# Hybrid decoder step: the value half of the gated MLP projected with stationary weights, and brought back to tokens by 32x32 transposes and DRAM

## The chip, the cores and the metric

The kernel runs on one core of one Trainium2 chip. Its time is the device time of one execution in microseconds (us). The core has five instruction streams: TensorE (PE; its weight loads are shown apart as PEld), VectorE (DVE), ScalarE (ACT), GpSimd (POOL) and SyncE (SP). Each works through its own list in order, and they wait for each other by semaphores. DMA transfers are issued from the lists of SP, ACT and POOL.

## The reference

One layer over 320 tokens (256 of a prompt, 64 of eight samples), width 2048, float32. What matters here is the input projection and the gated MLP:

```python
h = rms_norm(x, p["norm_mix_pre"])
proj = h @ p["w_in"]            # columns: gMLP u | gMLP v | SSD z | SSD x,B,C | SSD dt
...
u = jax.nn.gelu(a_u, approximate=False)
v = layer_norm(jax.nn.gelu(a_v, approximate=False), ln_g, ln_b)   # over 2048 columns
s = jnp.einsum("hts,bnshd->bnthd", w, vp) + b_s ...               # mixes tokens of a chunk
return u * s, v[:, start:]
```

`a_v` is h times 2048 columns of `w_in`. Its layer norm runs over columns, and the spatial gate contracts over tokens, so the kernel wants v with tokens on the partitions: `vt`, 128 partitions x 3 chunks of tokens (128, 128 and 64) x 2048 columns. Everything else it keeps with columns on the partitions and the 320 tokens along the free dimension.

## The kernel before

**Products in three parts.** A float32 operand is split in two, a rounded high part and the residue (hi, lo), and a product is the sum of three matmuls: high x high, low x high, high x low. x comes with columns on the partitions; `h_hi` and `h_lo` hold its parts for all 16 blocks of 128 input columns (`kt`).

**Weights.** `slab` (L109) loads up to 128 x 1024 weights (512 KB) on SP's queue into `wraw`; ACT casts them to `whi` (L123) and DVE makes the residue `wlo` (L124). Each of the three tiles has three buffers. A load therefore waits until the residue of the slab three back is made, and a cast until PE is done with the slab three back. `wraw` is shared with two loads of the dt columns (`wraw_dt`, `dt_columns`).

**The usual projection.** `project` (L194) takes 512 columns at a time: four PSUM banks, one per block of 128 columns; weights stationary (128x128), 320 tokens streaming; 3 x 16 matmuls of 320 per block (`accumulate`, L150 to L155). A block is evacuated by a callback when its last matmul is made. There are four banks with the tag `mm`, so a block of the next project waits for the evacuation of the block of the same number.

**The projection of v.** It comes first in the program, and the other way round: tokens stationary, weights streaming. `by_tokens` (L131, matmuls at L143) makes for each `kt` and each half (n = 0, 1; 1024 columns each) 16 matmuls of 512 columns: two chunks of 128 tokens x two groups x three products, and for the 64 tokens of the samples two matmuls per group with both parts of x side by side (`xs_two`, 2 x 64 columns, made by DVE at L646), one of them with 64 stationary columns. PSUM holds 3 x 2 banks per half. At the end of a half ACT takes Gelu straight from PSUM into `vt`, scaled by the RMS factor of each token (L721); for the samples DVE first adds the two parts (L719, L720). The first half (n = 0) runs while x arrives. In the same steps `x_ready` (L634) splits x (ACT L639, DVE L640), `x_squares` (L648) squares it on ACT (L651) and adds on DVE (L653), `root` makes the RMS factor r, and `dt_products` (L518) projects dt. In the second half `spread` turns r into r1 (one row per partition), and `params` loads `prm` and `sst` on SP.

**After v.** B, C and the first heads (`conv_proj`, L460) are projected with the usual `project`. Beside them `layer_norm` (L727) runs in pieces: `bn_stats` on 512 columns at a time (L734), `bn_aggr`, and two passes over `vt` (L752, L753), 24 in all. `gate_mix` (L765) then uses `vt` as stationary operand (L786).

**What sets the order.** Background work is written as generators. `tick` is called after each part of a `project`; it advances every task in `side` and the first in `bg`. What a generator yields is the number of matmuls until it may go on. A scheduler then orders each engine's list by priorities (`first()` and `high_priority` go ahead; `issue_after` holds an instruction behind another one). `pv` is a tag with four buffers of 128 x 320, shared by several short-lived tiles; `vf` has two of 128 x 4 x 320.

## Time and profile before

| | |
|---|---|
| Runs, us | 1768.35, 1768.94, 1769.97 (median 1768.94) |
| The profiled execution, us | 1768.21 |
| Its span, first to last instruction, us | 1766.5 |
| Mean granted TensorE clock | 0.999 |
| PE busy | 1754.9 us (99%) |
| DVE, ACT, POOL busy | 1171.0, 823.7, 286.4 us |
| First v matmul, first matmul of B | 5.42 us, 128.24 us |

In a row of a group of instructions stand the line in the kernel, the engine, the operation, the tiles as out<-in, the shapes and the count; behind the bar the busy time in us, the mean duration of one in ns, and the idle time of the engine ahead of it with what ended it. Matmuls are pipelined: the next one starts while the one before is still in flight, so a duration says how long one is in flight, and the distance of the starts what one costs. In a row of waits stand who waited, for whom, the us in total, the times, and the longest. In a row of a window stand the stretch, the busy time and count of PE, PEld, DVE, ACT and POOL, the granted clock, the share of time in which the DMA engines were busy, and GB/s. In a row of DMA issues stand out<-in, the queue, the count, the size of one, and the median us from issue to landing.

### The profile page before, as it was taken

How to read it: one execution, taken by the hardware profiler on the slowest of the kernel's cores; microseconds unless marked ns; L12 is line 12 of the kernel's file. 1: busy time of each engine (PE TensorE's matmuls, PEld its weight loads, DVE VectorE, ACT ScalarE, POOL GpSimd, SP SyncE). 2: the span in 40 equal slices, each digit the busy share in tenths (PEclk: the TensorE clock that was granted, in tenths of full speed). 3: DMA queues.
4: the chain of work that ended last, by engine and by line, in shares of the span. 5: the costliest groups of instructions: out<-in, count | busy, mean ns of one | idle time of the engine just before them, and what ended most of it. 6: DMA issues, size and time to landing. Idle time of an engine off the chain costs nothing.

```text
span 1766.5 us, 30627 instructions
## 1 busy us (share of the span) xinstructions
PE 1754.9 (99%) x11873; PEld 1708.2 (97%) x11873; DVE 1171.0 (66%) x2020; ACT 823.7 (47%) x1200; POOL 286.4 (16%) x627
## 2 busy tenths in 40 slices
PE   9999999999999999999999999999999999999998
PEld 7789999999899999999999999999999999999998
DVE  7549774656869777788855565665657565656575
ACT  5434555333655575655645434343434343333445
POOL 1202220000313222112211111010202010101004
PEclk9999999999999999999999999999999999999999
DMA  7556655455676766665654545554554545454542
GB/s 261 161 153 169 192 167 160 149 153 156 213 224 181 238 199 210 199 208 162 186 155 146 157 146 157 146 157 146 156 148 154 150 152 150 153 156 145 155 152 103
DMA packets 221051, 296.97 MB, mean 168 GB/s; under 512 B 19945, under 2 KB 147305, under 8 KB 220713
## 3 DMA queue, kind: packets, MB, share of 16 engines
q1 hardware_dynamic: 208568, 274.61, 51.5%
q10 hardware_dynamic: 9584, 13.38, 2.1%
q0 software_dynamic: 2752, 7.02, 1.4%
q8 instruction: 94, 1.54, 0.4%
q14 instruction: 53, 0.43, 0.1%
HBM read 277.88 MB, written 17.07 MB: 167 GB/s over the span
## 4 chain that ended last, share of the span: by engine, by line
PE 60%; DVE 0%; ACT 0%; issue 0%; ACTq 0%
PE ps L153 12%; PE ps L155 12%; PE ps L154 12%; PE pd L155 7%; PE pd L154 7%; PE pd L153 7%; PE x1p L1381 0%; PE fin_ps L1111 0%; PE y_ps L1039 0%; PE tsum L311 0%; PE ps_one L153 0%; PE ps_one L155 0%; PE ps_one L154 0%; PE ps_other L153 0%; PE ps_other L155 0%; PE ps_other L154 0%
## 5 line engine op out<-in xcount | busy, mean ns | idle before, releaser
L124 DVE TENSOR_TENSOR wlo<-wraw,whi 128x1024 fp32r<-128x1024 f32 (+1 forms) x476 | 582.6, 1224 | 427.0 <-ACT whi L123 424.7
L123 ACT CAST whi<-wraw 128x1024 fp32r<-128x1024 f32 (+1 forms) x475 | 494.7, 1042 | 676.2 <-PE ps L154 333.3
L153 PE MATMUL ps<-h_hi,whi 128*128 128x320 f32 x2268 | 700.7, 309 | 1.0 <-ACT whi L123 0.7
L155 PE MATMUL ps<-h_hi,wlo 128*128 128x320 f32 x2268 | 698.6, 308 | 0.7 <-DVE wlo L124 0.7
L154 PE MATMUL ps<-h_lo,whi 128*128 128x320 f32 x2268 | 699.1, 308 | 0.0
L153 PEld LDWEIGHTS ps<-h_hi,whi 128*128 128x128 f32 x2268 | 425.5, 188 | 4.1 <-issue 1.2
L155 PEld LDWEIGHTS ps<-h_hi,wlo 128*128 128x128 f32 x2268 | 425.5, 188 | 1.0 <-DVE wlo L124 1.0
L154 PEld LDWEIGHTS ps<-h_lo,whi 128*128 128x128 f32 x2268 | 425.7, 188 | 0.4
L155 PE MATMUL pd<-fhi,wlo 128*128 128x320 f32 x704 | 217.0, 308 | 0.0
L153 PE MATMUL pd<-fhi,whi 128*128 128x320 f32 x704 | 217.0, 308 | 0.0
L154 PE MATMUL pd<-flo,whi 128*128 128x320 f32 x704 | 217.0, 308 | 0.0
L153 PE MATMUL pd<-ohi,whi 128*128 128x320 f32 x448 | 138.9, 310 | 1.3 <-DVE pad L474 1.3
L155 PE MATMUL pd<-ohi,wlo 128*128 128x320 f32 x448 | 138.3, 309 | 0.0
L154 PE MATMUL pd<-olo,whi 128*128 128x320 f32 x448 | 138.3, 309 | 0.0
L153 PEld LDWEIGHTS pd<-fhi,whi 128*128 128x128 f32 x704 | 132.1, 188 | 0.0
L154 PEld LDWEIGHTS pd<-flo,whi 128*128 128x128 f32 x704 | 132.1, 188 | 0.0
L155 PEld LDWEIGHTS pd<-fhi,wlo 128*128 128x128 f32 x704 | 132.1, 188 | 0.0
L1283 POOL COPY ptf<-pad 128x2 f32<-128x2 f32 x88 | 21.0, 238 | 600.0 <-DVE pad L1271 599.4
L266 DVE TENSOR_TENSOR acc_ffn<-acc_ffn,pd 128x320 f32<-128x320 f32 (+1 forms) x161 | 77.5, 482 | 37.8 <-PE pd L155 36.4
L153 PEld LDWEIGHTS pd<-ohi,whi 128*128 128x128 f32 x448 | 84.1, 188 | 2.4 <-issue 1.3
L154 PEld LDWEIGHTS pd<-olo,whi 128*128 128x128 f32 x448 | 84.1, 188 | 0.3
L155 PEld LDWEIGHTS pd<-ohi,wlo 128*128 128x128 f32 x448 | 84.1, 188 | 0.0
(337 smaller groups left out, 1868.0 us busy)
## 6 DMA issues: line engine op xcount, KB each, us to landing
wraw<-in_ffn_w_up SPq DMA_DIRECT2D x176, 512.0 KB, 3.7
wraw<-in_w_in SPq DMA_DIRECT2D x140, 512.0 KB, 3.8
wraw<-in_ffn_w_down SPq DMA_DIRECT2D x88, 512.0 KB, 3.4
wraw<-in_w_out SPq DMA_DIRECT2D x64, 512.0 KB, 3.4
st<-in_state_ssm SPq DMA_DIRECT2D x40, 256.0 KB, 4.8
out_ssm_state_sample<-st ACTq DMA_DIRECT2D x30, 256.0 KB, 2.6
cs<-dacs_d SPq DMA_DIRECT2D x16, 320.0 KB, 5.1
xr<-in_xT SPq DMA_DIRECT2D x4, 640.0 KB, 4.1
```

The costliest lines, as they stand in the source:

```text
L123: rounded[:] = [act.copy(hi, raw).ins]
L124: dve.tensor_tensor(out=lo, in0=raw, in1=hi.bitcast(F32), op=ALU.subtract)
L153: pe.matmul(ps, whi, xhi, start=first, stop=False)
L154: pe.matmul(ps, whi, xlo, start=False, stop=False)
L155: last_made[0] = pe.matmul(ps, wlo, xhi, start=False, stop=last).ins
L266: added_last[:] = [dve.tensor_tensor(out=acc[:, nb, ts], in0=acc[:, nb, ts], in1=ps[:, ts], op=ALU.add).ins]
L1283: pool.tensor_copy(ptf[:, k, :], pad[:, 256:258])
```

## The change

v is projected like everything else: weights stationary, the 320 tokens streaming, as 16 blocks of 128 columns in 3 x 16 matmuls each. `by_tokens`, `banks` and `xs_two` go.

- The first six blocks (768 columns) take the place of the first half, beside the arrival of x. A slab is 768 columns wide (two of 384 in the first four steps), and a step has 18 matmuls of 320. The six banks are four of `mm` and two of `ms`.
- The other ten blocks are two projects of 512 columns and one of 256.
- `v_out` evacuates a block: DVE transposes its 32x32 squares from PSUM into `turned` (two tiles of the tag `vf`, each for two pairs of blocks). After every second block POOL stores the pair to DRAM (`v_d`) in four DMAs, one for each 32 partitions, with runs of 64 floats.
- `v_in`, a task in `side`, loads a pair back with tokens on the partitions (`v_rows`, tag `pv`, three DMAs on POOL). 48 matmuls later three Gelus on ACT (one per chunk of tokens) write 256 columns of `vt` in their right order, and after every second pair DVE makes `bn_stats` of 512 columns.
- `spread`, `params` and the first step of the dt task become a background task. `layer_norm` waits until `v_in` is done, and then makes `bn_aggr` and its two passes as before.

In the changed kernel lines move: the cast and the residue stay at L123 and L124, the three products are L134 to L136, h_lo is L622, the adds of squares L633, the Gelu of v L679, the transposes L657, the stores L661 and the loads L675.

**DVE in the x stage.** Rows of DVE's list before, from the residue of kt = 6 to that of kt = 8 (wlo is a slab's residue, h_lo that of x, acc_mix the sum of squares, w_dt the scaled dt columns):

```order
L124 TENSOR_TENSOR wlo<-wraw,whi 128x1024
L640 SCALAR_TENSOR_TENSOR h_lo<-vt,h_hi 128x320
L646 COPY xs_two<-h_hi 128x64
L653 TENSOR_TENSOR acc_mix<-acc_mix 128x640
L646 COPY xs_two<-h_lo 128x64
L653 TENSOR_TENSOR acc_mix<-acc_mix 128x640 x2
L124 TENSOR_TENSOR wlo<-wraw,whi 128x1024
L640 SCALAR_TENSOR_TENSOR h_lo<-vt,h_hi 128x320
L646 COPY xs_two<-h_hi 128x64
L510 TENSOR_TENSOR w_dt<-wraw_dt,vt 128x256
L646 COPY xs_two<-h_lo 128x64
L124 TENSOR_TENSOR wlo<-wraw,whi 128x1024
```

In the changed kernel, from the residue of kt = 7 to that of kt = 10:

```order
L124 TENSOR_TENSOR wlo<-wraw,whi 128x768
L622 SCALAR_TENSOR_TENSOR h_lo<-vt,h_hi 128x320
L492 TENSOR_TENSOR w_dt<-wraw_dt,vt 128x256
L124 TENSOR_TENSOR wlo<-wraw,whi 128x768
L622 SCALAR_TENSOR_TENSOR h_lo<-vt,h_hi 128x320
L633 TENSOR_TENSOR acc_mix<-acc_mix 128x640 x3
L124 TENSOR_TENSOR wlo<-wraw,whi 128x768
L622 SCALAR_TENSOR_TENSOR h_lo<-vt,h_hi 128x320
L633 TENSOR_TENSOR acc_mix<-acc_mix 128x640
L124 TENSOR_TENSOR wlo<-wraw,whi 128x768
```

The copies into xs_two are gone, the residues are 768 wide, and three adds of squares with an h_lo now stand directly ahead of the residue of kt = 9.

**ACT where v's Gelus stand.** Before, from the last casts of the first half (the Gelus read PSUM, `ps_v`, or the sample sums in `acc_mix`):

```order
L123 CAST whi<-wraw 128x1024 x3
L721 ACTIVATE vt<-ps_v,rs_r 128x512 x4
L123 CAST whi<-wraw 128x1024
L721 ACTIVATE vt<-acc_mix,rs_r 64x512 x2
L123 CAST whi<-wraw 128x1024 x3
L321 COPY r_115<-spread 128x320
L123 CAST whi<-wraw 128x1024 x12
L721 ACTIVATE vt<-ps_v,rs_r 128x512 x4
```

In the changed kernel, from the first cast of the seventh block on (the Gelus read `v_rows`, which a DMA brings):

```order
L123 CAST whi<-wraw 128x1024 x4
L302 COPY r_123<-spread 128x320
L123 CAST whi<-wraw 128x1024 x6
L679 ACTIVATE vt<-v_rows,rs_r 128x256 x2
L679 ACTIVATE vt<-v_rows,rs_r 64x256
L679 ACTIVATE vt<-v_rows,rs_r 128x256
L123 CAST whi<-wraw 128x1024
L679 ACTIVATE vt<-v_rows,rs_r 128x256
L679 ACTIVATE vt<-v_rows,rs_r 64x256
L123 CAST whi<-wraw 128x1024 x2
L679 ACTIVATE vt<-v_rows,rs_r 128x256 x2
L679 ACTIVATE vt<-v_rows,rs_r 64x256
```

Two groups of six Gelus of 512 columns have become eight groups of three of 256, each between weight casts; the chunks of the second pair stand on both sides of a cast.

**POOL behind the first blocks.** Before, from the clearing of vt's sample rows on (`lg` and `lb` are the rows of the layer norm's weights, `r_there` marks r1):

```order
L713 MEMSET vt 64x2048
L471 COPY pad<-sst 128x8x3 x3
L405 COPY r_there<-r_115 128x1
L745 DMA lg<-in_gate_ln_g 128x512
L745 DMA lb<-in_gate_ln_b 128x512
L524 COPY dtf<-dtf 128x64
L526 COPY dtf<-dtf 128x128 x2
L745 DMA lg<-in_gate_ln_g 128x512
L745 DMA lb<-in_gate_ln_b 128x512
```

In the changed kernel, from the same place on (`v_d_106` is the first pair in DRAM, `v_d_107` the second):

```order
L724 MEMSET vt 64x2048
L661 DMA v_d_106<-turned 32x10x64 x4
L661 DMA v_d_107<-turned 32x10x64 x4
L661 DMA v_d_108<-turned 32x10x64 x4
L675 DMA v_rows<-v_d_106 128x256 x2
L675 DMA v_rows<-v_d_106 64x256
L387 COPY r_there<-r_123 128x1
L506 COPY dtf<-dtf 128x64
L508 COPY dtf<-dtf 128x128 x2
L675 DMA v_rows<-v_d_107 128x256
L760 DMA lg<-in_gate_ln_g 128x512
L661 DMA v_d_109<-turned 32x10x64
```

Twelve stores and the first loads of v now stand ahead of r_there, and the later stores and loads stand between the loads of lg and lb.

The diff, cut to its core:

```diff
+    v_d = [dr.tile([NT, 2 * P], F32, name=f"v_d{i}") for i in range(KD // 2)]
...
-                        for i in range(2):
-                            dve.tensor_copy(xs_two[kt // 8][:, kt % 8, NS * i:NS * i + NS], hT[i][:, kt, NP:])
...
-            for n in range(2):
-                ps = banks("ps_v")
-                for kt in range(KD):
-                    x = [h[:, kt, :] for h in hT], xs_two[kt // 8][:, kt % 8, :]
...
-                        wb = slab(rows_of(w_in, kt, 1, cs, 1024))
-                        by_tokens(ps, *x, [wb(0, g, 512) for g in range(2)], (0, 1), kt == 0, kt == KD - 1)
...
+            turned = [gp.tile([P, 4, NT], F32, tag="vf", name="turned", bufs=2).rearrange("p j n -> p (j n)") for _ in range(2)]
+            turned = [t[:, 2 * NT * h:2 * NT * h + 2 * NT].rearrange("p (s j f) -> p s j f", j=2, f=32) for t in turned for h in range(2)]
+            v_there = []
+
+            def v_out(b, ps):
+
+                t = turned[b // 2 % len(turned)]
                 with first():
-                    for c, g in ((0, 0), (0, 1), (1, 0), (1, 1), (2, 0), (2, 1)):
-                        at, src = slice(0, NS if c == 2 else P), ps[c][g]
-                        if c == 2:
-                            src = acc[:, 2 + 2 * g:4 + 2 * g, :].rearrange("p k n -> p (k n)")[:NS, :512]
-                            dve.tensor_copy(src, ps[2][g][NS:])
-                            dve.tensor_tensor(out=src, in0=src, in1=ps[2][g][:NS], op=ALU.add)
-                        func_ins.append(act.activation(vt[at, c, 1024 * n + 512 * g:1024 * n + 512 * g + 512], src[at], AF.Gelu,
-                                                       scale=r[at, c:c + 1]).ins)
-
-            with tc.issue_after(func_ins[-1]):
-                act.activation(held, ones[:, 0:1], AF.Silu)
+                    dve.transpose(out=t[:, :, b % 2], in_=ps[:, :NT].rearrange("p (s f) -> p s f", f=32))
+                if b % 2:
+                    for i in range(4):
+                        rs = slice(32 * i, 32 * i + 32)
+                        pool.dma_start(v_d[b // 2][:, 64 * i:64 * i + 64].rearrange("(s t) e -> t s e", t=32),
+                                       t[rs].rearrange("p s j f -> p s (j f)"))
+                    v_there.append(b // 2)
+
+            bn = [gp.tile([P, 4, 6], F32, name=f"bn{c}") for c in range(3)]
+
+            def v_in():
+
+                for a in range(KD // 2):
+                    while a not in v_there:
+                        yield 24, 0
+                    rows = []
+                    for c, (o, n) in enumerate(TOK):
+                        rows.append(tp.tile([P, NT], F32, tag="pv", name="v_rows", bufs=4)[:, :2 * P])
+                        pool.dma_start(rows[c][:n], v_d[a][o:o + n])
+                    yield 48, 0
+                    with tc.issue_after(last_made[0]):
+                        for c, (o, n) in enumerate(TOK):
+                            func_ins.append(act.activation(vt[:n, c, 2 * P * a:2 * P * a + 2 * P].rearrange("p (j i f) -> p j i f", j=2, f=32),
+                                                           rows[c][:n].rearrange("p (i j f) -> p j i f", j=2, f=32), AF.Gelu, scale=r[:n, c:c + 1]).ins)
+                            if a % 2:
+                                dve.bn_stats(bn[c][:n, a // 2, :], vt[:n, c, 256 * a - 256:256 * a + 256])
+                    yield 0, 0
+            ps = [mm.tile([P, 512], F32, tag="mm", name=f"ps_v{j}") for j in range(4)] + [misc(f"ps_v{j}") for j in (4, 5)]
+            for kt in range(KD):
+                x_ready(kt, 1)
+                x = [h[:, kt, :] for h in hT]
+                if kt < 4:
+                    for g in range(2):
+                        wb = slab(rows_of(w_in, kt, 1, V0 + 384 * g, 384), g, begins=kt + g == 0)
+                        if kt == 0:
+                            made_so_far[0] += 9
+                            for i in (0, 2, 1):
+                                for j in range(3):
+                                    pe.matmul(ps[3 * g + j][:, :NT], wb(0, j)[i // 2], x[i % 2], start=i == 0, stop=False)
+                        else:
+                            for j in range(3):
+                                accumulate(ps[3 * g + j][:, :NT], wb(0, j), *x, False, False)
+                else:
+                    wb = slab(rows_of(w_in, kt, 1, V0, 768))
+                    for j in range(6):
+                        accumulate(ps[j][:, :NT], wb(0, j), *x, False, kt == KD - 1)
...
+            for j in range(6):
+                v_out(j, ps[j])
...
+            def with_r1():
+                spread(r, r1)
+                with_r1_there()
+                yield 24, 0
+                params()
+                for q in range(4):
+                    rs = slice(32 * q, 32 * q + 32)
+                    pool.tensor_copy(sums[rs, 0], ident[rs, rs])
+                next(tasks)
+                yield 24, 0
+            bg.append(with_r1())
+            v_task = v_in()
+            side.append(v_task)
+            project(w_in, V0 + 768, lambda j, ps: v_out(6 + j, ps))
+            project(w_in, V0 + 1280, lambda j, ps: v_out(10 + j, ps))
+            project(w_in, V0 + 1792, lambda j, ps: v_out(14 + j, ps), width=256)
 
             def layer_norm():
 
                 mv = gp.tile([P, 3, 2], F32, name="mv")
                 pool.memset(mv, 1.0)
+                while v_task in side:
+                    yield 24, 0
                 for c, (o, n) in enumerate(TOK):
-                    st = gp.tile([P, 4, 6], F32, tag="bn", name="bn", bufs=2)
-                    for q in range(4):
-                        dve.bn_stats(st[:n, q, :], vt[:n, c, 512 * q:512 * q + 512])
-                    dve.bn_aggr(mv[:n, c, :], st[:n].rearrange("p a b -> p (a b)"))
-                    yield
+                    dve.bn_aggr(mv[:n, c, :], bn[c][:n].rearrange("p a b -> p (a b)"))
```

71 lines of the change are left out of this document (19 added, 52 removed).

## The prediction

> **What bounds the kernel now.** I read the page first: busy time, granted clock, chain of waits.
>
> ```profile
> PE 1754.9 (99%) x11873; PEld 1708.2 (97%) x11873; DVE 1171.0 (66%) x2020; ACT 823.7 (47%) x1200; POOL 286.4 (16%) x627
> PEclk9999999999999999999999999999999999999999
> PE 60%; DVE 0%; ACT 0%; issue 0%; ACTq 0%
> ```
>
> TensorE (PE) is never idle for long, its clock is full throughout, and the chain that ends last names hardly anything but PE. So the time is the sum of the spacings of PE's instructions, and a change of 0.2% (3.5 us, about what a measurement of this kernel can tell from no change) has to come from PE's own stream or from a new wait of PE. Next the stage that is edited, by its tile, by the waits up to 130 us (first row) and up to 330 us (the other two):
>
> ```profile
> L143 PE MATMUL ps_v<-whi,h_hi x128: 387/392/662, 5.4 to 126.6; 128*128 128x512 f32 x128
> L143 PE MATMUL ps_v<-whi,h_lo x128: 387/393/404, 6.1 to 126.8; 128*128 128x512 f32 x128
> L143 PE MATMUL ps_v<-wlo,h_hi x128: 390/393/404, 6.8 to 127.1; 128*128 128x512 f32 x128
> L143 PE MATMUL ps_v<-whi,xs_two x64: 388/396/398, 6.6 to 128.0; 128*128 128x512 f32 x64
> L143 PE MATMUL ps_v<-wlo,xs_two x64: 388/397/399, 7.3 to 127.8; 128*64 128x512 f32 x64
> ...
> PEld ps_v L143 <- issue: 0.5, 1, 0.5
> ...
> DVE wlo L124 <- ACT whi L123: 93.0, 49, 5.0
> ACT whi L123 <- PE ps_v L143: 60.4, 26, 5.2
> ```
>
> 512 matmuls of 512 columns run from 5.4 to 128.2 us, and PE waits in them for 0.5 us. The weight casts wait for PE (60.4 us): the weights are ahead.
>
> **PE's own work.** A duration of 393 ns is not a cost, since neighbours overlap; the spacing is. Four windows (busy time and count of PE, PEld, DVE, ACT, POOL; clock; DMA share; GB/s):
>
> ```profile
> 5.00:20.00 15.00, 15.00 (x66) 11.89 (x66) 13.23 (x33) 11.70 (x20) 2.25 (x7) 1.00 1.00 361
> 20.00:40.00 20.00, 20.00 (x88) 15.61 (x87) 15.43 (x31) 10.98 (x15) 0.00 (x0) 1.00 0.68 219
> 65.00:125.00 60.00, 60.00 (x262) 46.85 (x261) 24.89 (x25) 21.18 (x24) 6.17 (x16) 1.00 0.56 170
> 155.00:183.00 28.00, 28.00 (x193) 28.00 (x192) 25.30 (x45) 13.31 (x22) 10.57 (x21) 1.00 0.72 214
> ```
>
> Some two matmuls straddle the edges and are counted, so the third row holds 257.3 v matmuls beside three short transposes (the spread, 0.4 us): 59.6/257.3 = 231.6 ns. The fourth row is the projection of C, with the shape that v gets: 28.0/191 = 146.6 ns. Per column 320 is no better than 512; the gain comes from the columns. The old form streams 512 x 512 = 262,144 of them (the sample chunk has 64 tokens but pays for two of its three products as full matmuls), the new one 768 x 320 = 245,760. Before: 512 x 231.6 = 118.6 us. After: 768 x 146.6 = 112.6 us. **Gain 6.0 us.** The dt product, the token sums and the spread stay on PE.
>
> The Trainium skill ("TensorE: Matmul & The Clock Gate", "Back-to-back issue gap") gives a gap of N/2.4 + 2.5 ns, warm: 215.8 and 135.8 ns, by which the gain would be 6.2 us. Both rows lie above it, by 16 and 11 ns; the measured ones decide.
>
> **The x stage (first six blocks): can ACT, DVE and the loads keep up?** One step of 128 input rows falls from 16 x 231.6 = 3.71 us to 18 x 146.6 = 2.64 us. Weights per step fall by a quarter too, but x is split and squared at the same amount per step. Durations, from the groups in 5.4 to 128.2 us:
>
> ```profile
> L640 DVE SCALAR_TENSOR_TENSOR h_lo<-vt,h_hi 128x320 fp32r<-128x320 f32 x16 | 8.9, 556 | 0.0
> L639 ACT ACTIVATE h_hi<-vt 128x320 fp32r<-128x320 f32 x15 | 8.4, 560 | 0.0
> L653 DVE TENSOR_TENSOR acc_mix<-acc_mix 128x640 f32<-128x640 f32 x7 | 5.8, 822 | 0.2
> L124 DVE TENSOR_TENSOR wlo<-wraw,whi 128x512 fp32r<-128x512 f32 x8 | 5.6, 704 | 0.2 <-ACT whi L123 0.2
> L721 ACT ACTIVATE vt<-ps_v,rs_r 128x512 f32<-128x512 f32 x8 | 5.5, 688 | 0.0
> L651 ACT ACTIVATE acc_mix<-vt 128x640 f32<-128x640 f32 x8 | 5.4, 723 | 0.0
> L123 ACT CAST whi<-wraw 128x512 fp32r<-128x512 f32 x7 | 4.3, 619 | 1.8 <-DMA wraw<-in_w_in 1.3 <-DMA vt<-in_xT 0.4
> L646 DVE CAST xs_two<-h_lo 128x64 fp32r<-128x64 f32 x16 | 3.1, 192 | 0.0
> ...
> L719 DVE COPY acc_mix<-ps_v 64x512 f32<-64x512 f32 x2 | 1.3, 690 | 0.0
> L720 DVE TENSOR_TENSOR acc_mix<-acc_mix,ps_v 64x512 f32<-64x512 f32 x2 | 1.3, 676 | 0.0
> ...
> L510 DVE TENSOR_TENSOR w_dt<-wraw_dt,vt 128x256 f32<-128x256 f32 x2 | 0.8, 423 | 0.5 <-DMA wraw_dt<-in_w_in 0.5
> ```
>
> ```profile
> L124 DVE TENSOR_TENSOR wlo<-wraw,whi 128x1024 fp32r<-128x1024 f32 (+1 forms) x476 | 582.6, 1224 | 427.0 <-ACT whi L123 424.7
> L123 ACT CAST whi<-wraw 128x1024 fp32r<-128x1024 f32 (+1 forms) x475 | 494.7, 1042 | 676.2 <-PE ps L154 333.3
> ```
>
> Halfway between their 512 and 1024 forms the 768-wide cast takes 0.83 us and the residue 0.96 us. In the eight steps with squares ACT then has 0.83 + 0.56 + 0.72 = 2.11 us of work and DVE 0.96 + 0.56 + 0.82 = 2.34 us, against 2.64: 80% and 89%, so neither is the bound on average. Tighter is the ring of three raw weight buffers: a load can start when the residue of the slab three back is made. Loads, by the DMA views of 8 to 30 us (first and third row) and of the whole run:
>
> ```profile
> wraw<-in_w_in SPq DMA_DIRECT2D x7, 512.0 KB, 4.1
> vt<-in_xT ACTq DMA_DIRECT2D x7, 320.0 KB, 5.4
> wraw_dt<-in_w_in SPq DMA_DIRECT2D x2, 512.0 KB, 4.5
> b_d<-turned POOLq DMA_DIRECT2D x20, 32.0 KB, 2.9
> b_raw<-b_d POOLq DMA_DIRECT2D x2, 256.0 KB, 3.5
> ```
>
> Load 4.1, cast 0.83, residue 0.96: 5.9 us for three slabs that PE eats in 7.9. The queue of DVE adds to it: in the new order three adds and an h_lo stand between one slab's cast and its residue, 3 x 0.82 + 0.56 = 3.0 us, so that one round takes 8.9 and loses 1.0. The two dt loads each take a buffer out of the ring; two buffers give a slab per 2.95 us, 0.3 over, for some three slabs, 0.9 each time. Cast weights lie up to two slabs (5.3 us) ahead and can absorb all of this. Bounds: nothing and 2.8 us. I take **0.7 us**, nearer to nothing since the weights were ahead in the rows above.
>
> **The way back to tokens.** POOL gets 32 stores and 24 loads; ACT gets 24 Gelus of 256 for twelve of 512; DVE gets 16 transposes of 320 out of PSUM for 32 x 0.19 of xs_two copies and 8 x 0.68 of sample sums. The nearest rows:
>
> ```profile
> L441 POOL DMA_DIRECT2D b_d<-turned x20 | 10.6, 538 | 2.0 <-DVE turned L439 2.0
> L439 DVE STREAM_TRANSPOSE turned<-bT 128x256 f32<-128x256 f32 x5 | 2.0, 422 | 1.2 <-DMA b_d<-turned 1.2
> L485 ACT ACTIVATE bT<-cv 128x256 f32<-128x256 f32 x4 | 1.7, 419 | 2.6 <-DVE cv L480 2.5
> ```
>
> POOL: 56 x 0.54 = 30 us on an engine that is 16% busy. ACT: 24 x 0.42 = 10.1 for 8.3 us. DVE: a transpose by 320/256 x 422 = 0.53 us (0.42 to 0.69 by L439 and L719), 8.5 for 11.5 us. All of it lies beside PE, unless an engine's queue stops. PE's next project needs the bank of block j when it reaches its own block j; the transpose has 0.88 us per block (six matmuls) for its 0.53, so the banks hold by themselves. Later than before are layer_norm's 24 passes, behind the last Gelus instead of from about 130 us; DVE was busy 25.3 of 28 us in 155 to 183 then, with PE never waiting, and its twelve bn_stats are spread out now. I allow **0.1 us** for a bank that is freed late (0 to 1).
>
> **Sum.** The profiled execution took 1768.2 us with a span of 1766.5, and lies 0.7 below the median of the runs, 1768.94. 1768.2 - 6.0 + 0.7 + 0.1 = 1763.0 for a profiled execution, and **1763.7 us** for the runs.
>
> **Rivals.**
> (a) The x stage becomes bound by the raw ring. For it: DMA is full (share 1.00) in 5 to 20 us, and the x loads took 5.4. With 5.4 for a weight load and one add and one h_lo in each round, a round is 5.4 + 1.79 + 1.38 = 8.6 us, 2.86 per slab, 0.22 over, for twelve whole slabs 2.6 us, and 0.9 for dt: 3.5 lost, 1768.94 - 6.0 + 3.5 = 1766.4 us. Against it: a slab is a quarter smaller, and PE waited nowhere in this stage.
> (b) Slower: the Gelus stop ACT. From the second pair on a pair's v_rows wait for the Gelus of the pair before (four pv buffers, three per pair), so between two groups lie three issues on POOL and a load, 1.6 + 3.5 = 5.1 us by the b_raw row, 7.0 at the x loads' 5.4. ACT is in order: a Gelu that waits holds the weight cast behind it. That cast has three slabs (10.6 us) less cast, residue and a Gelu group (1.05 + 1.22 + 1.3), 7.0 us; with the cast that stands between the groups PE waits from a round trip of some 8 us. At 10.5 us the four groups that follow closely (pairs 1, 4, 6, 7) would cost 4 x 2.5 = 10 us: 1768.94 - 6.0 + 10 = 1773 us. Against it: no POOL load in the rows is that slow. The Trainium skill ("DMA: Bandwidth & Descriptors", the table at its head) says that transfers under 512 B lose line rate; v_d is written in runs of 256 B, and no row here shows such a store. By that rule the stores land later than b_d's 2.9 us, but they stand ahead of this loop, not in it.
> (c) The change adds 256 weight loads. Were they not hidden, 256 x 188 ns (the mean of LDWEIGHTS) would cost 48 us: 1811 us. The Trainium skill (same TensorE page, "What overlaps and what doesn't") says they overlap running matmuls only in other row groups; by this rule it would be so. Against it, decisively: C's matmuls have a new full-height load each and start every 146.6 ns, less than one load's 188.
>
> ```profile
> L153 PEld LDWEIGHTS ps<-h_hi,whi 128*128 128x128 f32 x2268 | 425.5, 188 | 4.1 <-issue 1.2
> ```
>
> **How the numbers follow.** Forecast, the stalls within 2.3 us: 70%, 1762 to 1765.4 us. (a): 20%, 1765.4 to 1769. (b): 7%, 1772.5 and more. (c): 1%. Remaining 2%: the stalls of PE that lie later, after 440 us, move, within 0.2%. Above 3.5 us gained is faster: 70%. Within 0.2%: 20 + 2 = 22%. Slower: 8%. The range leaves out (b), (c) and the worst of (a): 1761.5 (no stall, and a first slab of 192 KB that starts PE a little earlier) to 1768.5.
>
> **What would show it.** PE's first matmul of B (128.24 us before) comes at about 123. The six blocks of the x stage end near 50 us, with waits of PE on wlo between steps 6 and 10 if the ring is tight; under (a) they are there in most steps. In B and C the spacing is 146.6 ns. Under (b) the wait of whi on vt or v_rows is long and PE waits on ACT between 75 and 135 us. If PE's stream is not 6 us shorter from 5.4 us to B, the first term is wrong; if it is and the time is not, look behind 440 us.

## The result, and the profile after

The changed kernel takes 1764.13 us (median of 9 runs, 1762.62 to 1766.17) against 1768.35 us for the kernel before beside it (1767.00 to 1770.57): a ratio of 0.9976, 95% interval 0.9967 to 0.9986, that is 4.2 us faster. The prediction said 1763.7 us. The profiled execution took 1763.86 us, its span 1762.2 us, 4.3 us less than before.

The page of the changed kernel: busy time, granted clock, chain of waits.

```profile
PE 1751.7 (99%) x12129; PEld 1730.0 (98%) x12129; DVE 1170.2 (66%) x2000; ACT 826.8 (47%) x1216; POOL 321.8 (18%) x683
PEclk9999999999999999999999999999999999999999
PE 90%; DVE 4%; DMA 3%; issue 1%; ACT 1%; POOL 1%; SPq 0%; ACTq 0%; POOLq 0%; DVEq 0%
```

PE still bounds the kernel. The shares of this chain can't be set against those of the chain before: that one reaches back only to 692.6 us, and so says nothing of the stage that is edited. The windows of the stages that the prediction used:

```profile
5.00:20.00 15.00, 15.00 (x100) 15.00 (x100) 9.66 (x19) 8.27 (x16) 2.08 (x8) 1.00 0.97 328
20.00:40.00 20.00, 18.71 (x123) 17.75 (x122) 16.54 (x25) 14.45 (x23) 3.00 (x4) 1.00 0.68 190
60.00:120.00 60.00, 60.00 (x411) 60.00 (x410) 28.34 (x32) 23.96 (x32) 25.04 (x48) 1.00 0.81 239
```

From 60 to 120 us, where v's later blocks run, some two of the 411 matmuls straddle the edges: 60.0/409 = 146.7 ns each, the spacing that was forecast, with a full-height weight load each. From 5 to 20 us the DMA engines are full (0.97), as before. Between 20 and 40 us PE does nothing for 1.3 us. Where it stops, by the waits of 5 to 50 us:

```profile
ACT whi L123 <- DMA wraw<-in_w_in: 11.5, 9, 3.9
...
DVE w_dt L492 <- DMA wraw_dt<-in_w_in: 2.9, 2, 1.6
...
PEld ps_v L136 <- DVE wlo L124: 2.2, 4, 1.3
PE ps_v L136 <- DVE wlo L124: 1.2, 2, 1.0
```

Four waits of PE for wlo, in steps 6, 7, 8 and 9 of the x stage. Against a spacing of 146.7 ns, with the restart behind each, they cost 0.17, 0.36, 0.45 and 1.29 us, 2.27 in all. The chain that ended last, from 0 to 60 us, says what was late (start, duration, what):

```profile
8.88 4.31 DMA wraw<-in_w_in
13.29 0.85 ACT whi L123
14.17 0.97 DVE wlo L124
15.15 5.05 DMA wraw<-in_w_in
20.31 0.85 ACT whi L123
21.18 0.97 DVE wlo L124
22.16 4.74 DMA wraw_dt<-in_w_in
26.93 0.44 DVE w_dt L492
27.38 3.27 DMA wraw<-in_w_in
```

This is one of the three raw buffers going round: load, cast, residue, and at once the next load into the same buffer. One of its rounds, 22.16 to 27.38, carries dt and not a slab: 5.2 us in which this buffer brings PE nothing. Up to 27.38 the chain can be followed in this buffer. Behind it, it can't: the load of 27.38 brings step 10's slab, while the chain goes on with the residue at 31.19, which is step 9's, in another buffer. What held steps 7 to 9 is read from the timelines of VectorE and of ACT:

```profile
26.93 0.42 DVE L492 TENSOR_TENSOR w_dt<-wraw_dt,vt 128x256 f32<-128x256 f32 x1 [1.33 <-DMA wraw_dt<-in_w_in]
27.27 0.95 DVE L124 TENSOR_TENSOR wlo<-wraw,whi 128x768 fp32r<-128x768 f32 x1
28.14 0.55 DVE L622 SCALAR_TENSOR_TENSOR h_lo<-vt,h_hi 128x320 fp32r<-128x320 f32 x1
28.60 2.67 DVE L633 TENSOR_TENSOR acc_mix<-acc_mix 128x640 f32<-128x640 f32 x3
31.19 0.95 DVE L124 TENSOR_TENSOR wlo<-wraw,whi 128x768 fp32r<-128x768 f32 x1
```

```profile
23.95 0.82 ACT L123 CAST whi<-wraw 128x768 fp32r<-128x768 f32 x1
...
28.46 0.83 ACT L123 CAST whi<-wraw 128x768 fp32r<-128x768 f32 x1 [1.34 <-DMA wraw<-in_w_in]
```

Step 8's slab was there, and its cast was done at 24.8 us. Its residue came only at 27.27, because in VectorE's list it stands behind the product with dt, and VectorE waited 1.33 us for dt. Step 9's slab was late (ACT waited 1.34 us for it), and behind its cast, which ended at 29.29 us, the three adds of the squares (2.67 us) still ran ahead of its residue. So dt in the ring acts in two ways: it takes slots that bring no slab, and its own load has to wait for a slot, so that VectorE stands at dt and the residues behind it are late. The adds come on top. Both suspects of the prediction, the ring with dt in it and the queue of adds, are at work; the experiments tell how much each is worth.

The way back, by the tiles v_d and v_rows, and the only wait of ACT, PE or VectorE for it between 55 and 130 us:

```profile
L661 POOL DMA_DIRECT2D v_d<-turned x32: 598/601/639, 53.0 to 128.9; - x32
L675 POOL DMA_DIRECT2D v_rows<-v_d x24: 534/551/577, 60.1 to 134.8; - x24
DMA to landing us min/median/max: 2.2/4.1/5.9
```

```profile
ACT vt L679 <- DMA v_rows<-v_d: 4.5, 3, 1.9
```

ACT waits three times, 1.9 us at most, and PE has no row in that view. PE's first matmul of B starts at 124.47 us (128.24 before): 6.0 us of stream less 2.3 of stalls. The other 0.5 us of the 4.3 came behind 440 us, where waits moved (below).

### The profile page after: what moved, and what is told of

It is laid out like the page before. It is cut to its first block, busy times and chain, and to the rows that moved or that the text cites. A ratio compares the mean times of both kernels' runs of the same rounds, so it can differ in the third digit from the quotient of the medians.

```text
span 1762.2 us, 31244 instructions
## 1 busy us (share of the span) xinstructions
PE 1751.7 (99%) x12129; PEld 1730.0 (98%) x12129; DVE 1170.2 (66%) x2000; ACT 826.8 (47%) x1216; POOL 321.8 (18%) x683
## 4 chain that ended last, share of the span: by engine, by line
PE 90%; DVE 4%; DMA 3%; issue 1%; ACT 1%; POOL 1%; SPq 0%; ACTq 0%; POOLq 0%; DVEq 0%
PE ps L134 18%; PE ps L135 18%; PE ps L136 18%; PE pd L134 10%; PE pd L135 10%; PE pd L136 10%; DVE wlo L124 1%; DMA wraw<-in_w_in 1%; PE y_ps L1054 1%; DMA st<-in_state_ssm 1%; DMA wraw<-in_ffn_w_up 1%; ACT whi L123 0%; PE sg L801 0%; PE up_ps L990 0%; POOL st L984 0%
## 5 line engine op out<-in xcount | busy, mean ns | idle before, releaser
L124 DVE TENSOR_TENSOR wlo<-wraw,whi 128x1024 fp32r<-128x1024 f32 (+2 forms) x480 | 581.9, 1213 | 420.6 <-ACT whi L123 418.7
L123 ACT CAST whi<-wraw 128x1024 fp32r<-128x1024 f32 (+2 forms) x479 | 495.7, 1035 | 664.3 <-PE ps L135 376.6
L134 PE MATMUL ps<-h_hi,whi 128*128 128x320 f32 x2428 | 751.0, 310 | 0.9 <-ACT whi L123 0.8
L136 PE MATMUL ps<-h_hi,wlo 128*128 128x320 f32 x2428 | 748.6, 309 | 0.7 <-DVE wlo L124 0.7
L135 PE MATMUL ps<-h_lo,whi 128*128 128x320 f32 x2428 | 749.1, 309 | 0.0
L134 PEld LDWEIGHTS ps<-h_hi,whi 128*128 128x128 f32 x2428 | 456.2, 188 | 4.2 <-issue 1.2
L136 PEld LDWEIGHTS ps<-h_hi,wlo 128*128 128x128 f32 x2428 | 456.3, 188 | 1.0 <-DVE wlo L124 1.0
L135 PEld LDWEIGHTS ps<-h_lo,whi 128*128 128x128 f32 x2428 | 456.5, 188 | 0.4
L136 PE MATMUL pd<-fhi,wlo 128*128 128x320 f32 x704 | 217.0, 308 | 0.0
L134 PE MATMUL pd<-fhi,whi 128*128 128x320 f32 x704 | 217.0, 308 | 0.0
L134 PE MATMUL pd<-ohi,whi 128*128 128x320 f32 x448 | 138.9, 310 | 0.5 <-DVE pad L456 0.5
L136 PE MATMUL pd<-ohi,wlo 128*128 128x320 f32 x448 | 138.3, 309 | 0.0
L134 PEld LDWEIGHTS pd<-fhi,whi 128*128 128x128 f32 x704 | 132.2, 188 | 0.0
L136 PEld LDWEIGHTS pd<-fhi,wlo 128*128 128x128 f32 x704 | 132.2, 188 | 0.0
L134 PEld LDWEIGHTS pd<-ohi,whi 128*128 128x128 f32 x448 | 84.1, 188 | 1.6 <-PE pd L136 0.9
L136 PEld LDWEIGHTS pd<-ohi,wlo 128*128 128x128 f32 x448 | 84.1, 188 | 0.0
```

Source lines behind the costliest of these rows:

```text
L123: rounded[:] = [act.copy(hi, raw).ins]
L124: dve.tensor_tensor(out=lo, in0=raw, in1=hi.bitcast(F32), op=ALU.subtract)
L134: pe.matmul(ps, whi, xhi, start=first, stop=False)
L135: pe.matmul(ps, whi, xlo, start=False, stop=False)
L136: last_made[0] = pe.matmul(ps, wlo, xhi, start=False, stop=last).ins
```

## The experiments

Ratios are to the kernel before on the same chip, with 95% intervals; a single run has none. "Waits" are PE's and PEld's rows for ps_v on wlo or whi between 5 and 50 us (PEld counts the longer); the 0.5 us of PEld behind the dt product, which every kernel has, is not counted.

| kernel | waits, us | B begins, us | time, us | ratio |
|---|---|---|---|---|
| before | 0 | 128.24 | 1768.35 | 1 |
| changed | 2.2 | 124.47 | 1764.13 | 0.9976 (0.9967 to 0.9986) |
| e1 adds on POOL | 5.5 | 127.03 | 1767.16 | 0.9990 (0.9982 to 0.9999) |
| e2 dt late | 0 | 122.23 | 1762.88 | 0.9970 (0.9958 to 0.9981) |
| e3 both | 4.3 | 126.64 | 1767.20 | 0.9991 (0.9982 to 1.0000) |
| e4 no way back | 3.3 | 124.90 | 1766.20 | 0.9986 (0.9977 to 0.9995) |
| e5 dt's own buffers, product late | 0 | 121.93 | 1760.17 | one run |
| e6 dt's own buffers, product in place | 0 | 122.38 | 1762.72 | one run |
| e7 one more hop | 2.9 | 124.93 | 1767.76 | 0.9997 (0.9988 to 1.0006) |
| e8 e2, b on ACT's queue | 0 | 122.38 | 1763.90 | 0.9974 (0.9963 to 0.9984) |
| e9 no adds | 1.3 | 123.24 | 1763.56 | one run |
| e10 e5, timed | 0.2 | 122.70 | 1763.59 | 0.9961 (0.9947 to 0.9974) |
| e11 e10, b plain | 0.5 | 122.61 | 1759.10 | 0.9940 (0.9927 to 0.9954) |
| e12 e10, b copied ahead | 1.0 | 122.28 | 1758.80 | 0.9942 (0.9928 to 0.9955) |

**e1: the adds on POOL.**

```diff
-                    dve.tensor_tensor(out=acc[:, 0:2, :], in0=acc[:, 0:2, :], in1=sq, op=ALU.add)
+                    pool.tensor_tensor(out=acc[:, 0:2, :], in0=acc[:, 0:2, :], in1=sq, op=ALU.add)
```

> The seven adds of the squares go from VectorE to POOL; nothing else. In the changed kernel PE loses some 2.3 us in the x stage, each time on wlo: 0.17 us in step 6, 0.36 in step 7, 0.45 in step 8, 1.29 in step 9. Theory Q (VectorE's queue: adds that stand between a cast and its residue): the waits of steps 7 and 9 go, those of 6 and 8 stay, B begins about 1.6 us earlier, at 122.8 us, and the time falls by 1.6 us against the changed kernel. Theory L (the raw ring: two buffers taken by dt and loads of 4 to 5 us): the residues wait for the loads anyway, B begins at 124.1 or later and the time falls by less than 0.4 us.

Neither theory had this: the waits grew to 5.5 us. The groups of e1 between 26 and 36 us:

```profile
L633 POOL TENSOR_TENSOR acc_mix<-acc_mix 128x640 f32<-128x640 f32 x6 | 11.5, 1915 | 0.5
L622 DVE SCALAR_TENSOR_TENSOR h_lo<-vt,h_hi 128x320 fp32r<-128x320 f32 x3 | 5.6, 1858 | 0.0
L124 DVE TENSOR_TENSOR wlo<-wraw,whi 128x768 fp32r<-128x768 f32 x2 | 4.6, 2301 | 0.0
```

and the same of the changed kernel:

```profile
L124 DVE TENSOR_TENSOR wlo<-wraw,whi 128x768 fp32r<-128x768 f32 x4 | 3.8, 951 | 0.0
L622 DVE SCALAR_TENSOR_TENSOR h_lo<-vt,h_hi 128x320 fp32r<-128x320 f32 x3 | 1.6, 545 | 0.0
```

While POOL adds, VectorE's residue takes 2.30 us for 0.95 and h_lo 1.86 for 0.55: 1.3 us more each, on VectorE, which was to be relieved. The Trainium skill ("SBUF — State Buffer", "SBUF: two separate sides") says that VectorE with two inputs from SBUF and GpSimd hold one port pair in turn, each for a whole instruction; the rows agree with it. So e1 says nothing on the two theories, and e3 neither.

**e2: dt behind the squares.**

```diff
-                if kt in (5, 8):
-                    dt_columns(kt // 8)
+                if kt in (11, 12):
+                    dt_columns(kt - 11)
...
-                if kt == 13:
+                if kt == 14:
                     dt_products()
```

> The two dt loads and products of VectorE with them go from steps 5 and 8 to steps 11 and 12 (the dt product on PE one step later), behind the squares; adds stay on VectorE. Theory L: the ring has its three buffers back in steps 6 to 9, all of the 2.3 us goes, B begins at 122.2 us. Theory Q: step 8's wait (VectorE stands at w_dt until dt's load has landed, 1.3 us) and step 6's go, 0.6 us; the adds still delay a residue, so 1.2 us or more stays, B at 123.5 or later; and nothing new at steps 11 to 14.

By e2's waits of 5 to 50 us PE waits for no weight at all, and the window of 20 to 40 us is full:

```profile
PEld ps_v L134 <- issue: 0.5, 1, 0.5
DVE w_dt L492 <- DMA wraw_dt<-in_w_in: 0.5, 1, 0.5
```

```profile
20.00:40.00 20.00, 20.00 (x138) 20.00 (x137) 16.25 (x25) 13.61 (x22) 2.19 (x4) 1.00 0.66 189
```

B begins at 122.23 us, 6.01 us before the old kernel's 128.24. That is theory L, and with nothing waiting it is also the first term of the prediction by itself: 6.0 us. That the two agree to 0.01 us is luck: the other kernels without such a wait begin B 5.86 us (e6, e8) and 6.31 us (e5) before the old one, since in each execution PE's first matmuls run at half the clock (267 ns apart) for a shorter or longer time. The adds still stand on VectorE, two at most between a cast and its residue, and cost nothing. The runs alone (0.9970 against 0.9976, intervals that overlap) do not separate e2 from the changed kernel; B's start does.

**e3: both edits.**

> Both edits. Either theory: no wait of PE over 0.1 us in the x stage, B begins at 122.2 us (6.0 us before the old kernel's 128.2, which is the first term of the prediction alone), and the time is 2.3 us below the changed kernel's, unless the stalls behind 430 us take it back. If B begins at 122.2 and the end gains less than 1.5 us, the rest is lost at 430 to 560 us, where the state loads are waited for.

B begins at 126.64 us with 4.3 us of waits: POOL's adds slow VectorE here as in e1. A miss, and no test of the sum.

**e4: without the way back.**

```diff
-                        pool.dma_start(v_d[b // 2][:, 64 * i:64 * i + 64].rearrange("(s t) e -> t s e", t=32),
-                                       t[rs].rearrange("p s j f -> p s (j f)"))
+                        pass
...
-                        rows.append(tp.tile([P, NT], F32, tag="pv", name="v_rows", bufs=4)[:, :2 * P])
-                        pool.dma_start(rows[c][:n], v_d[a][o:o + n])
+                        rows.append(turned[a % len(turned)][:, 0:4].rearrange("p s j f -> p (s j f)"))
```

> Leaves out v_d: the 32 stores and 24 loads on POOL are gone and the Gelus read a slice of the turned tile, so the v that comes out is not v; PE, the transposes and the 24 Gelus stay. Theory H (the way back is hidden): B begins within 0.2 us of the changed kernel's 124.5 and the time is within 0.4 us of it. Rival (its DMAs delay weight slabs or its waits stop ACT): B or the first wait behind it comes 0.5 us or more earlier.

B begins at 124.90 us, 0.43 later, because the x stage lost 3.4 us in this execution (step 6 alone 1.3 instead of 0.17), while PE was earlier by 0.7 us when it came to step 6. From the dt product, where that stage's waits are over, to B it takes 124.90 - 46.49 = 78.41 us; in the changed kernel 124.47 - 46.06 = 78.41. The way back costs PE nothing up to there. The time is not lower, even 0.1% higher, and the expectation of 0.4 us was missed: behind B PE lost 0.5 us more at 155 us and 1.0 more at 437 us than in the changed kernel. The Gelus of e4 wait for no DMA and come earlier; that this moves what lies behind B is a guess, which no run tests.

**e5 and e6: two buffers of dt's own**, loads issued where the changed kernel has them, the products late (e5) or in place (e6). Core of e6:

```diff
-                raw = wp.tile([P, 1024], F32, tag="wraw", name="wraw_dt", bufs=3)
+            raw_dt = [gp.tile([P, 4, NT], F32, tag="vf", name="wraw_dt", bufs=2).rearrange("p j n -> p (j n)")[:, :1024] for _ in range(2)]
```

> The dt loads are issued on SP where the changed kernel has them (behind the slabs of steps 5 and 8), but into two buffers of their own (the tag that the turned tiles use later), and VectorE's products with them stand at steps 11 and 12 as in e2. So no buffer is taken out of the ring and VectorE never waits for dt, but the bytes still move in 12 to 27 us. Theory L1 (the two ring buffers and VectorE's wait at w_dt): no wait of PE, B begins at 122.2 us. Rival L2 (DMA bandwidth: 1 MB more in a time of full DMA): slabs land late, PE waits 0.5 us or more in steps 6 to 9.

> As e5, but VectorE's products stand behind the residues of steps 5 and 8 as in the changed kernel, so that VectorE, which is in order, waits there until dt has landed. If the buffers taken from the ring are the cause, B begins at 122.2 us; if VectorE's wait is, the residues behind it come late and PE waits about as in the changed kernel (1 to 2.3 us in all, B at 123.2 to 124.5).

No wait in either; B at 121.93 and 122.38 us. The megabyte of dt still moves within the x stage, though a little earlier: its loads are issued at 10.8 and 17.6 us in e5, and at 12.5 and 22.2 in the changed kernel, where they wait for a slot. In steps 7 to 9 neither kernel loses anything, so there the bytes of dt by themselves (theory L2) are not what takes the time. For step 6 L2 stays open: in e10, the same kernel as e5, and in e12 the slab of step 6, which is issued behind dt's first load, was cast as late (20.65 and 20.21 us) as in the changed kernel (20.31), and in e5 and e6 earlier (18.46 and 18.34). In e6 VectorE waited for dt only 0.6 us where the changed kernel has 2.9, for the loads no longer wait for a buffer of the ring; so e6 excludes the place of the products as a cause by itself, not a long wait there. What takes the time in steps 7 to 9 is dt in the ring, through the slots that it takes and through VectorE's wait for it; no run parts these two.

**e10: e5 again, timed.**

> The kernel of e5 again, now timed: dt in two buffers of its own, products of VectorE with it behind the squares. B at 121.9 us again, 6.3 us before the old kernel's, and a time 6 to 8 us below the old kernel's, 0.9955 to 0.9966 of it, which is 2 to 3 us below the changed kernel's.

0.9961, inside the expected 0.9955 to 0.9966; B at 122.70 us, 0.8 later than in e5, with the first six matmuls at half the clock and 0.2 us of wait in step 6. Its interval still overlaps the changed kernel's. e5's one run, 1760.17 us, lies below all five of e10's (1761.83 to 1764.12), though the kernel is the same: the time of one run says little here.

**e9: no adds at all**, dt in the ring.

```diff
-                if kt:
-                    dve.tensor_tensor(out=acc[:, 0:2, :], in0=acc[:, 0:2, :], in1=sq, op=ALU.add)
```

> Leaves out the seven adds of the squares (so the row scales are wrong); the dt loads stay in the ring. e1 could not tell this, since its adds on POOL made VectorE itself slow. If the ring is the whole cause, PE still waits about 2.3 us on wlo in steps 6 to 9 and B begins at 124 us or later. If the queue of adds is needed beside the ring (three adds stand between the cast and the residue of step 9), the wait of step 9 (1.3 us) and that of step 7 shrink to 0.3 us together and B begins at 122.8 to 123.3 us.

The waits of steps 7 and 9 are gone; those of step 6 (0.5 us with its restart) and of step 8 (0.8) stay. VectorE in e9:

```profile
27.00 0.42 DVE L492 TENSOR_TENSOR w_dt<-wraw_dt,vt 128x256 f32<-128x256 f32 x1 [1.91 <-DMA wraw_dt<-in_w_in]
27.34 0.95 DVE L124 TENSOR_TENSOR wlo<-wraw,whi 128x768 fp32r<-128x768 f32 x1
28.21 0.55 DVE L622 SCALAR_TENSOR_TENSOR h_lo<-vt,h_hi 128x320 fp32r<-128x320 f32 x1
29.23 0.96 DVE L124 TENSOR_TENSOR wlo<-wraw,whi 128x768 fp32r<-128x768 f32 x1 [0.48 <-ACT whi L123]
```

Step 9's residue starts at 29.23 instead of 31.19. In steps 7 to 9 PE loses 0.83 us without the adds and 2.10 with them. This loss needs dt in the ring: out of it, e2, e5 and e6 lose nothing in these steps with all adds in place. Step 6 is another matter (0.50 us here, 0.17 in the changed kernel; see what stays open).

**e7: a longer way back.**

```diff
-                        pool.dma_start(rows[c][:n], v_d[a][o:o + n])
+                        pool.dma_start(v_e[a][o:o + n], v_d[a][o:o + n])
+                        pool.dma_start(rows[c][:n], v_e[a][o:o + n])
```

> The way back takes one more copy through DRAM (v_d to a second tile, from which v_rows is loaded): 24 more DMAs on POOL. In the changed kernel ACT waited for v_rows 1.9 us at most (before 85.6 and before 106.8) and PE not at all. Three more issues at 0.55 us and one more flight of 2.5 to 3 us make these waits some 4.5 us longer. By rival (b) of the prediction PE waits from a round trip of 8 us on; this one has 9 to 10, so PE waits 1 to 2 us at two to four places between 75 and 135 us, 2 to 8 us in all, the time 1766 to 1772. If the cover is wider than worked out there, PE waits nowhere and B begins within 0.5 us of the changed kernel's 124.5.

From the dt product to B it is again 78.41 us (46.52 to 124.93): between 75 and 125 us 24 more DMAs and a longer flight cost PE nothing, so the cover is wider there than rival (b) had it. It gives way once, behind the last pair. ACT and DVE in e7:

```profile
147.19 1.22 DVE L124 TENSOR_TENSOR wlo<-wraw,whi 128x1024 fp32r<-128x1024 f32 x1 [2.30 <-ACT whi L123]
...
150.49 1.33 ACT L681 ACTIVATE vt<-v_rows,rs_r 128x256 f32<-128x256 f32 x3 [3.33 <-DMA v_rows<-v_e]
...
151.83 1.28 ACT L687 ACT_TABLE_LOAD   x1
```

A Gelu waits 3.33 us, the table load for Silu follows, the next cast begins at 153.24, its residue holds VectorE until 155.53, and the emptying of PE's bank stands behind that: PE loses 1.6 us at 155 to 157 (intervals of 1.44 and 0.49 us for 0.147). So (b)'s mechanism exists, at one place and for 1.6 us, not at four for 10. The time, 1767.76, lies 3.6 us above the changed kernel's. The profiled executions differ by 3.5 us: 0.5 of it is there at the start of B, 1.7 comes at 155 to 157 us, 1.5 at 559 us, where PE waited 1.65 us, and the rest nearly cancels.

**e8, e11, e12: what holds PE at 434 to 446 us.** All kernels above lose 1.1 to 2.8 us there on whi and wlo, and up to 2.3 more on the state loads. e8 put b's two loads on ACT's queue:

```diff
-                sp.dma_start(b4[i], b_d[o:o + 32].unsqueeze(0).broadcast_to([4, 32, 512]))
+                act.dma_start(b4[i], b_d[o:o + 32].unsqueeze(0).broadcast_to([4, 32, 512]))
```

> e2, and the two loads of B for the sample rows (b from b_d) go from SP's queue to ACT's. In all kernels so far a slab issued behind them at 424 to 428 us landed 10 us later, as did five state loads; PE lost 1.9 to 2.1 us on whi and wlo there and up to 2.1 us at the state loads. Theory: those two loads hold up SP's queue; without them the slab lands in 4 to 6 us, the two waits on whi and wlo (1.9 us in e2) go, and the time falls by 1.5 to 3.5 us below e2's. Rival: the transfers share the same DMA engines in either queue, and nothing moves.

ACT in the changed kernel shows what PE waited for at 434 to 438 us:

```profile
431.05 0.62 ACT L860 CAST bsp<-b 128x512 fp32r<-128x512 f32 x1 [2.87 <-DMA b<-b_d]
435.89 0.62 ACT L860 CAST bsp<-b 128x512 fp32r<-128x512 f32 x1 [4.22 <-DMA b<-b_d]
436.41 1.99 ACT L123 CAST whi<-wraw 128x1024 fp32r<-128x1024 f32 x2
```

The first of the two casts at 436.41 is of a slab that had been issued at 420.43 us, ahead of b, and had landed 3.8 us later. It was late because it stands behind the two casts of b in ACT's list, at which ACT waited 7.1 us for b's loads. PE's waits on whi and wlo come from there, and not from a slab that is loaded behind b.

In e8 that slab's cast stands ahead of the casts of b (427.53 us), and PE's waits at 434 us went, though ACT waited for b as long as before (7.3 us). The slab issued behind b landed after 12.1 us all the same, so SP's queue is not what makes it late. A wait of 3.2 us at 453 us came instead, for a bank that VectorE emptied late. No gain over e2.

e11 leaves the queue and changes what is read: 128 rows of b that follow each other, which are not the right ones, in place of 32 rows four times.

```diff
-                sp.dma_start(b4[i], b_d[o:o + 32].unsqueeze(0).broadcast_to([4, 32, 512]))
+                sp.dma_start(b4[i], b_d[P * i:P * i + P])
```

> As e10, but the two loads of b take 128 different rows of b_d instead of 32 rows four times (same bytes; the sample rows' B is wrong by it). If the fourfold reading is what holds the DMA queues at 424 to 437 us, the slab issued behind lands in 4 to 6 us instead of 10 to 12, PE's waits on whi and wlo at 434 us (1.1 us) and on the state (2.0 us) go, and the time falls by 1 to 3 us below e10's; or, as in e8, one wait behind them takes their place. If it lands as late as before, something else holds it.

1759.10 us, 4.5 less than e10, where 1 to 3 were expected. b lands after 2.9 us, the slab behind it after 5.9 (10.3 in e10), and PE's waits for whi and wlo and for the state loads at this place are gone. In e12 the right rows are copied beforehand:

```diff
+            for at in range(8):
+                o = NP + 32 * (at // 4)
+                pool.dma_start(b4_d[32 * at:32 * at + 32], b_d[o:o + 32])
...
+                sp.dma_start(b4[i], b4_d[P * i:P * i + P])
```

> e10, and the sample rows of b_d are copied four times into a DRAM tile of their own (8 DMAs of 64 KB on POOL at about 257 us, where nothing waits for them), so that the two loads of b at 423 us read 128 different rows, as in e11, but the right ones. If e11's reading holds: the slab issued behind them lands in about 6 us instead of 10, PE's waits at 434 to 436 us (2.1 us in e10) and at the state loads (2.2 us) go, one of 1.4 us before 550 us may stay, and the time is that of e11, 0.993 to 0.9955 of the old kernel's, 8 to 12 us below it and 4 to 7 us below the changed kernel's. If the eight copies disturb the slabs at 257 to 265 us, PE waits there and part of it is lost.

DMA issues with their landing, 422 to 438 us, in the changed kernel:

```profile
st<-in_state_ssm SPq DMA_DIRECT2D x5, 256.0 KB, 10.8
b<-b_d SPq DMA_DIRECT2D x2, 256.0 KB
wraw<-in_w_in SPq DMA_DIRECT2D x1, 512.0 KB, 10.4
```

and in e12, with its window of 425 to 452 us:

```profile
st<-in_state_ssm SPq DMA_DIRECT2D x8, 256.0 KB, 5.8
wraw<-in_w_in SPq DMA_DIRECT2D x2, 512.0 KB, 5.4
...
b<-b_d SPq DMA_DIRECT2D x2, 256.0 KB, 2.8
```

```profile
425.00:452.00 27.00, 27.00 (x203) 25.31 (x202) 21.93 (x33) 16.82 (x34) 12.58 (x12) 1.00 0.71 230
```

b lands after 2.8 us, so ACT no longer stands at its casts; the slab behind it lands in 5.4 us instead of 10.4, and PE is never idle in these 27 us. A short window of the changed kernel shows the slow read at work, 76 GB/s at a DMA share of 0.21:

```profile
426.00:428.00 2.00, 2.00 (x14) 2.00 (x15) 2.00 (x5) 2.00 (x5) 0.00 (x0) 1.00 0.21 76
```

The Trainium skill ("DMA: Bandwidth & Descriptors", "Rules for kernel authors") says that an outermost dimension of c under 16, such as a leading broadcast of c copies, confines a DMA to at most c engines. c is 4 here, and 4 of 16 engines would be a share of 0.25 by that page, an estimate; the row's 0.21 agrees. e12 is the fastest kernel here that computes what the reference does: 1758.80 us, 0.9942 (0.9928 to 0.9955), an interval that lies wholly below the changed kernel's.

## Why the prediction was right, step by step

- **PE's stream, 6.0 us: right.** The spacing is 146.7 ns; where nothing waits (e2) B begins 6.01 us earlier. The 256 more weight loads cost nothing. The prediction weighed two rules of the Trainium skill ("TensorE: Matmul & The Clock Gate") there. By the formula of "Back-to-back issue gap", which that section gives for a single matmul by itself, the spacings would be 215.8 and 135.8 ns and the gain 6.2 us; the rows have 231.6 and 146.7 ns. By "What overlaps and what doesn't" the prediction worked out a loss of 48 us; no such loss came, and loads of 188 ns each stay hidden under a spacing of 146.7 ns. The rows bear out neither.
- **The x stage, 0.7 us: the mechanism right, the size wrong.** It measured 2.3, inside the bounds (0 to 2.8) and near the end that was not taken. The durations were right (the residue of 768 took 951 ns for 0.96 us). The failed step is the choice: "nearer to nothing since the weights were ahead in the rows above". They were ahead of a PE that took 3.71 us per step; at 2.64 PE had to wait for them from step 6 on. The prediction also priced dt at "two buffers give a slab per 2.95 us" while dt's bytes move. e2, e5 and e6 show dt in the ring as the condition of the loss in steps 7 to 9, and e9 gives the sizes: 0.8 us with dt alone and 1.3 more with the adds, where the prediction's upper bound had 1.8 for the ring and 1.0 for the queue of adds. That the slot which dt takes from 12.51 us (issue of its first load) to 18.9 us (end of VectorE's product with it) uses up the lead is likely, but not shown. The reading that the chain before "names hardly anything but PE" carried nothing for this stage, since that chain starts at 692.6 us.
- **Rival (a)** named the ring and put the loss at 3.5 us; the truth lies between it and the forecast, nearer to (a). Its own sign, waits in most steps, did not come: four steps, 6 to 9, as the forecast said.
- **A bank freed late, 0.1 us: nothing**, PE has no wait between 55 and 180 us.
- **The way back, nothing: right** (78.41 us with it, without it and with one more hop). Rival (b) over-estimated its reach; its stores to v_d in runs of 256 bytes landed after 4.0 us (median, by the trace's row), later than b's loads in e12 (2.8), and without cost to PE. (c) did not occur.
- **Behind 440 us** the prediction expected no change. There 0.1 us more was lost on weights and 1.4 to a lower clock (last section), the wait for the state loads shrank from 1.8 to 0.2, the old kernel's wait of 1.2 us at 558 us went, and others, of 0.2 to 0.4 us, took back some 0.7: 3.77 us of lead at B are 4.3 at the end. So the x stage lost 1.6 us more than forecast, the bank 0.1 less, and 0.5 came back here: 1.0 us together, against the 0.9 between 1763.0, forecast for a profiled execution, and 1763.9. That the forecast came as near to the median as 0.4 us (1763.7 and 1764.1) is in part luck: the x stage was put 1.6 us too low, and against it the bank and the part behind 440 us were put 0.6 too high together, and the step from a profiled execution to the median was taken as 0.7 and measured 0.3.

What stays open. Step 6 waits 0.17 us in the changed kernel's execution and 0.5 to 1.3 us in those of e1, e4, e7, e9 and e12. Part of it is on record: in the changed kernel PE's first matmuls ran at half the clock and it ended step 5 at 21.68 us, in the others at 20.8 to 21.4 us, so that it stood earlier before a slab that came at much the same time (cast at 20.0 to 20.8 us). What a slow start costs, step 6 gives back. Not explained is why the slab of step 6 is cast at 18.3 to 18.8 us in e5, e6 and e11 and at 20.2 to 20.7 us in e10 and e12. And whether the wait of 1.2 to 1.3 us at 550 us in e10 to e12 can be moved, no run tells; the kernel before has it too, at 558 us.

## What to carry to other kernels

When one engine's work per step shrinks, the slack of every ring that feeds it shrinks with it: a side load that borrows a slot of a small ring takes a whole round of that slot (5.2 us here), in which the ring brings nothing, so do not price it at its bytes alone. It also waits for its slot, so see what stands behind it in the list of the engine that waits for it. Let it go where nothing else is tight, or into a buffer that is idle. Do not read "never waited" in the old profile as slack without dividing it by the new step time. And a two-input operation moved from VectorE to POOL may cost VectorE more than it saves. And where PE waits for weights, read the list of the engine that casts them: what was late here, at 434 us, was its neighbour's load (b), not the slab.

## What the runs showed of the hardware, beyond what was expected

The granted clock fell to half for 3.4 us in some executions, behind waits that were short. In the changed kernel PE lost 0.94 and 0.86 us between 436 and 439 us, and then:

```profile
440.00:443.20 3.20, 3.20 (x14) 3.20 (x13) 2.45 (x3) 1.84 (x3) 0.00 (x0) 0.50 0.94 307
```

Twelve matmuls started every 267 ns instead of 147: 1.4 us, which here the state load would have made PE wait anyway. The kernel before had waits of 0.82 and 0.86 us at this place and kept its clock, e9 had 1.20 and 0.86 and kept it, e6 had 1.04 and 0.86 and lost it: their length alone does not decide. By the clock records of the traces the stretch of the changed kernel goes from 439.98 to 443.39 us. Every such stretch here is 3.41 us long and starts a whole number of 3.41 us behind the clock's first rise to full (127 of them in the changed kernel, 126 in e6, 132 in e8), so the clock seems to be set window by window. The Trainium skill ("TensorE: Matmul & The Clock Gate", "What's actually happening") puts the fall down to an idle window of 3.4 us that runs freely. The length of the stretch and its coming and going agree with such a window; that it has to be idle throughout does not, since PE worked for more than half of the window ahead of the fall (1.94 of 3.41 us). Nor does the idle time alone decide: 1.48 us of a window in the changed kernel and 1.58 in e6 were followed by the half clock, 1.45 in e10 and even 1.83 in e1 (28.5 to 31.9 us) were not. What decides stays open.

POOL's adds slowed VectorE's two-input operations by 1.3 us each (e1), and a read that names 32 rows four times kept slabs behind it for 5 us longer than one of 128 rows (10.4 and 5.4 us).
